# Branch b's eight output panels as seven products of halves per pair, in a one-layer streaming encoder

## The chip, the cores and the metric

The kernel runs on one core of a Trainium2 chip. The metric is the device time of one execution in microseconds (us), the median of several runs. The engines are TensorE (PE, with its weight loads PEld), VectorE (DVE), ScalarE (ACT), GpSimd (POOL), and SyncE (SP), whose queue issues most DMAs. An instruction waits in its engine's queue until what it needs is there, and all behind it wait with it.

## The reference

One layer with two branches. T = 1088 tokens (a prompt of 1024 and 64 sampled tokens), D = 1024 channels, all float32. Branch a gives `ya` (convolution, gated linear recurrence), branch b gives `yb` (forgetting attention). What the change concerns is the merge:

```python
ya = ya * jax.nn.silu(ga)
yb = yb.reshape(B, L, W_B) * jax.nn.silu(gb)
u = jnp.einsum('bsnw,nwd->bsnd', jnp.stack([ya, yb], axis=2), w_branch)
gates = jax.nn.sigmoid(jnp.stack([ma, mb], axis=2))
mix = jnp.sum(gates * u, axis=2) @ w_o
h = x + rms_norm(mix, g_post)
```

Each branch is multiplied by its own 1024 x 1024 matrix, gated per channel, the two are added, and the sum is multiplied by `w_o`.

## The kernel before

Activations lie transposed: channels on the 128 partitions in eight blocks (KT = 8), tokens along the free axis. An output panel is 128 output channels for all 1088 tokens, in three chunks of 368, 368 and 352 columns, each in one PSUM bank. Every float32 operand is split into a high and a low part (`wh`, `wl` for weights, `yah`, `yal` for inputs): ACT copies the high part, DVE subtracts it for the low part. A product is then three matmuls (`three`, L165 to L167: high by high, high by low, low by high), so a panel takes 3 chunks x 8 blocks x 3 = 72 matmuls.

Earlier in the program the q, k and gate panels are made differently. Two panels together are a product of 2 x 2 block matrices (halves of the tokens, of the input channels), made with seven products of halves instead of eight, as in Strassen's scheme in Winograd's form. One such product is 24 matmuls of 272 columns (L809, tile `quad`); POOL and DVE make the sums of the weights' halves (`split_pair`) and of the inputs' halves. Branches a and b do not use it.

The stage around the change, in the program's order:
- Branch a: panels 0 and 1 were begun earlier and are finished first (`finish_held`), then panels 2 to 7 (`panel_steps`). I call them a0 to a7. `evac_a` (L1900) multiplies each chunk by its sigmoid gate on DVE, and SP writes it to DRAM (`d_mix`).
- After each panel of a, `branch_b(of)` (L1870) makes one of the eight blocks of branch b's input: two loads, a sigmoid on ACT, a product on POOL (L1877), one on DVE (L1878), then the split into `ybh` and `ybl`.
- Branch b: eight panels of the same kind. `evac_b` gates each chunk, adds branch a's (`ma_in`, loaded from `d_mix`) and splits the sum into `mxh` and `mxl` in SBUF.
- `w_o` (`w_part`, 512 columns for each of nine blocks of tokens, the k-rows in two halves) reads `mxh` and `mxl`; then the last stage.

Weights come in pairs of panels (1 MB, four DMAs) into one raw buffer `w_raw` and are split a panel at a time into two rotating buffers (`wh`, `wl`). TensorE's order is the order of the code. In this stage a scheduler places the instructions of the other engines, from its own costs, and each engine then runs its list in order.

Of the kernel before, what the change touches and what calls it, by code (L numbers as in the profile page):

```python
# [67 lines left out]
def hybrid_step(tc, a, o):  # L68
# [31 lines left out]
    d_mix = dram.tile([KT, P, T], F32, name="d_mix")  # L100
    d_q = dram.tile([2, NP, P, T], F32, name="d_q")
# [107 lines left out]
    wpool = sb("wpool", bufs=2)  # L209

# [22 lines left out]
    for k in range(KT):  # L233
# [3 lines left out]
                  + [(w_br[i * D:(i + 1) * D, k * P:(k + 2) * P], ((t, k), (t, k + 1)))  # L237
                     for i, t in enumerate("ab") for k in range(0, KT, 2)])
# [574 lines left out]
    def keys_out(p, ss, c0, t0, blocks):  # L813
# [8 lines left out]
        for i, n in enumerate(blocks):  # L822
            n_st[0] += 1
            st = (wpool.tile([P, GC], F32, name="st") if n_st[0] % 3 else
# [1038 lines left out]
    xpool.close()  # L1863


    ybpool = sb("ybpool")
    yb = [tuple(ybpool.tile([P, T], F32R, name=f"yb{i}{k}") for i in "hl") for k in range(KT)]
    p4 = sb("p4", bufs=2)

    def branch_b(k):  # L1870
# [6 lines left out]
        pool.tensor_tensor(out=t[:, :], in0=t[:, :], in1=z[:, :], op=ALU.mult)  # L1877
        dve.tensor_tensor(out=t[:, :], in0=t[:, :], in1=s[:, :], op=ALU.mult)  # L1878
        h, l = yb[k]
        copy_act(h[:, :], t[:, :])  # L1880
        sub(dve, l[:, :], t[:, :], f(h[:, :]))

    def gate_in(pl, src):
        g = pl.tile([P, T], F32, name="gate", tag="gate", bufs=2)
        sp.dma_start(g[:, :], src)
        act.activation(out=g[:, :], in_=g[:, :], func=AF.Sigmoid)
        return g


    look_ahead()  # L1890
    split_next(dve, [t[:, :KT * P].rearrange("p (k n) -> p k n", k=KT) for t in yb[KT - 1]])
    g_next = gate_in(p4, d_ma[0])
    for of in range(KT):
        g = g_next
        if of + 1 < KT:
            g_next = gate_in(p4, d_ma[of + 1])

        def evac_a(c, t0, n, z):
            s = wpool.tile([P, GC], F32, name="st")
            dve.tensor_tensor(out=s[:, :n], in0=z, in1=g[:, t0:t0 + n], op=ALU.mult)  # L1900
# [4 lines left out]
        else:  # L1905
            tag, w = panel()
            assert tag == ("a", of)
            run(panel_steps(mm, *w, ya, evac_a))
        branch_b(of)
        if of == 2:  # L1910
            ft_p = mm.tile([P, 512], F32, name="ft_p", tag="acc")
            pe.transpose(ft_p[:64, :P], fin.rearrange("p s k -> p (s k)"), ident[:, :])
            ft = p4.tile([64, P], F32, name="ft", bufs=1)
            dve.tensor_copy(ft[:, :], ft_p[:64, :P])
# [4 lines left out]
    p4.close()  # L1919
    ypool.close()  # L1920

    NH2 = 2
    HW = D // NH2
    KH = KT // 2
    wq0 = sb("wq0", side="right")
    mxpool = sb("mxpool", side="right")
    p5 = sb("p5")
    mix = [tuple(mxpool.tile([P, T], F32R, name=f"mx{i}{of}") for i in "hl") for of in range(KT)]

    def mix_in(of):  # L1930
        g = gate_in(p5, d_mb[of])
        m = p5.tile([P, T], F32, name="ma_in", tag="ma_in", bufs=2)
        sp.dma_start(m[:, :], d_mix[of])
        return g, m

    def room_of(pl, raws, src, h, kh):

        wh = pl.tile([P, KH, HW], F32R, name="wqh", tag="wqh")
        wl = pl.tile([P, KH, HW], F32R, name="wql", tag="wql")
        for i in range(2):  # L1940
            k0 = KH * kh + 2 * i
            raw = raws[i] if raws is raw_half else raws.tile([P, KT * P], F32, name="wraw", tag="wraw", bufs=2)
            raw = raw.rearrange("p (k n) -> p k n", k=2)
            sp.dma_start(raw, src[k0 * P:(k0 + 2) * P, h * HW:(h + 1) * HW].rearrange("(k p) n -> p k n", p=P))
            ks_ = slice(2 * i, 2 * i + 2)
            copy_act(wh[:, ks_, :], raw)
            sub(dve, wl[:, ks_, :], raw, f(wh[:, ks_, :]))
        return wh, wl

    m_next = mix_in(0)  # L1950
    wo = {}
    for of in range(KT):
        g, ma_ = m_next
        if of + 1 < KT:
            m_next = mix_in(of + 1)

        def evac_b(c, t0, n, z):
            s = wpool.tile([P, GC], F32, name="st")
            c_ = slice(t0, t0 + n)
            dve.tensor_tensor(out=s[:, :n], in0=z, in1=g[:, c_], op=ALU.mult)  # L1960
            dve.tensor_tensor(out=s[:, :n], in0=s[:, :n], in1=ma_[:, c_], op=ALU.add)
            copy_act(mix[of][0][:, c_], s[:, :n])
            sub(dve, mix[of][1][:, c_], s[:, :n], f(mix[of][0][:, c_]))

        tag, w = panel()
        assert tag == ("b", of)
        if of == KT - 1:
            wo[0, 0] = room_of(wq0, raw_half, a["w_o"], 0, 0)
            wq0.tile([P, 56], F32, name="lead")
        run(panel_steps(mm, *w, yb, evac_b))  # L1970
    p5.close()
    ybpool.close()
    wpool.close()

# [3 lines left out]
    hpool = sb("hpool")  # L1978
    wq = sb("wq", bufs=3)
    tpool = sb("tpool")  # L1980
# [6 lines left out]
    wo[0, 1] = room_of(wq, tpool, a["w_o"], 0, 1)  # L1987
# [52 lines left out]
    wg = {}  # L2040
# [5 lines left out]
    def w_part(b, h, kh):  # L2046
# [4 lines left out]
        wh, wl = wo[h, kh]  # L2051
        for k in range(KH):
# [202 lines left out]
```

## Time and profile before

| | |
|---|---|
| median of 3 runs | 1424.47 us (1424.3 to 1426.01) |
| profiled execution, its span | 1425.84 us, 1424.0 us |
| TensorE clock granted | 0.998 |
| branch a's first panels finished | 1026.4 us into the span |
| branch b's first matmul | 1097.94 us |
| w_o's first matmul | 1192.66 us |

A line of a group has: source line, engine, operation, output <- inputs by name, shapes, number of instructions; then busy us and mean ns of one; then the engine's idle time before them and what ended it. A line of a timeline has: start, duration, engine, line, operation, and in brackets the idle time before it and its releaser. `SPq` is SP's queue issuing a DMA. A matmul's duration overlaps the next one's, so that rates are read from start to start.

### The profile page before, as it was taken

What the parts mean: (1) busy time and instruction counts of PE and PEld (TensorE: products, weight loads), DVE (VectorE), ACT (ScalarE), POOL (GpSimd) and SP (SyncE); (2) the same over time, 40 slices, a digit from 0 to 9 for tenths busy, and PEclk for the clock granted to TensorE, in tenths of its full rate; (3) what the DMA queues carried; (4) which work ended last, traced back from release to release, by engine and by line L of the source; (5) the groups of instructions that cost most, each with busy time, mean ns of one, the idle gap of its engine ahead of it and who ended that gap; (6) DMA issues with size and microseconds to landing.
All of it is one profiled execution on the core that took longest, in us unless ns stands there. A gap on an engine that the chain in (4) does not pass through costs nothing.

```text
span 1424.0 us, 23913 instructions
## 1 busy us (share of the span) xinstructions
PE 1407.3 (99%) x8967; PEld 1339.5 (94%) x8967; DVE 863.2 (61%) x1528; ACT 711.9 (50%) x1300; POOL 280.1 (20%) x370
## 2 busy tenths in 40 slices
PE   9999999999999999999999999999999999999997
PEld 8999999999999999999999989999999999888886
DVE  6546665665532467676676667799745544348644
ACT  5414444344321566666666657879533323324543
POOL 0001333413311333243432410010122000000001
PEclk9999999999999999999999999999999999999999
DMA  5376555656346857647465533331486534124111
GB/s 206 122 130 111 105 172 180 191 157 176 93 78 187 215 138 138 157 111 173 118 146 139 66 88 48 56 53 36 157 292 204 186 127 146 66 73 151 49 49 45
DMA packets 133552, 182.70 MB, mean 128 GB/s; under 512 B 22212, under 2 KB 97004, under 8 KB 133436
## 3 DMA queue, kind: packets, MB, share of 16 engines
q1 hardware_dynamic: 116892, 156.57, 44.0%
q10 hardware_dynamic: 16240, 23.97, 4.7%
q8 instruction: 71, 1.16, 0.3%
q0 software_dynamic: 304, 0.62, 0.1%
q14 instruction: 45, 0.37, 0.1%
HBM read 122.65 MB, written 58.46 MB: 127 GB/s over the span
## 4 chain that ended last, share of the span: by engine, by line
PE 90%; DMA 4%; DVE 3%; ACT 1%; issue 1%; SPq 0%; ACTq 0%; DVEq 0%
PE quad L809 19%; PE acc L165 15%; PE acc L166 15%; PE acc L167 15%; PE tp L1192 4%; PE s L1167 3%; PE s L1166 2%; PE pv L1221 2%; PE pv L1219 2%; DMA w_raw<-in_w_in 2%; PE vacc L165 1%; PE vacc L167 1%; PE vacc L166 1%; PE tp L2012 1%; DMA wv_raw<-in_w_in 1%
## 5 line engine op out<-in xcount | busy, mean ns | idle before, releaser
L165 PE MATMUL acc<-xh,wh 128*128 128x368 f32 (+1 forms) x672 | 227.6, 339 | 0.4
L166 PE MATMUL acc<-xl,wh 128*128 128x368 f32 (+1 forms) x672 | 219.9, 327 | 0.0
L167 PE MATMUL acc<-xh,wl 128*128 128x368 f32 (+1 forms) x672 | 219.6, 327 | 0.0
L165 PEld LDWEIGHTS acc<-xh,wh 128*128 128x128 f32 x672 | 126.4, 188 | 1.9 <-DVE nm L1146 1.3
L166 PEld LDWEIGHTS acc<-xl,wh 128*128 128x128 f32 x672 | 126.7, 189 | 0.6
L167 PEld LDWEIGHTS acc<-xh,wl 128*128 128x128 f32 x672 | 126.4, 188 | 0.0
L84 ACT ACTIVATE th<-tp 128x512 fp32r<-128x512 f32 (+1 forms) x160 | 86.7, 549 | 63.9 <-PE tp L1192 53.6
L87 DVE TENSOR_TENSOR tl<-tp,th 128x512 fp32r<-128x512 f32 (+1 forms) x160 | 99.2, 634 | 28.5 <-ACT th L84 27.4
L87 DVE TENSOR_TENSOR wl<-w_raw,wh 128x1024 fp32r<-128x1024 f32 (+1 forms) x64 | 73.0, 1140 | 60.6 <-ACT wh L84 51.2
L84 ACT ACTIVATE wh<-w_raw 128x1024 fp32r<-128x1024 f32 (+1 forms) x64 | 61.3, 959 | 94.9 <-PE quad L809 38.3
L1152 POOL TENSOR_SCALAR pb<-pb,sm 128x640 f32<-128x640 f32 (+1 forms) x64 | 61.6, 962 | 168.5 <-DVE sm L1151 153.4
L809 PE MATMUL quad<-xh,wh 128*128 128x272 f32 x448 | 94.0, 291 | 0.0
L809 PE MATMUL quad<-xl,wh 128*128 128x272 f32 x448 | 92.6, 288 | 0.0
L809 PE MATMUL quad<-xh,wl 128*128 128x272 f32 x448 | 92.5, 288 | 0.0
L1149 ACT ACTIVATE pb<-pb,nm 128x640 f32<-128x640 f32 (+1 forms) x64 | 63.3, 989 | 25.7 <-DVE nm L1146 17.7
L1219 PE MATMUL pv<-tl,vv 128*128 128x512 f32 x192 | 70.0, 365 | 2.1 <-DVE y L1231 1.3
L809 PEld LDWEIGHTS quad<-xl,wh 128*128 128x128 f32 x448 | 70.6, 188 | 0.0
L809 PEld LDWEIGHTS quad<-xh,wh 128*128 128x128 f32 x448 | 70.3, 188 | 0.2
L809 PEld LDWEIGHTS quad<-xh,wl 128*128 128x128 f32 x448 | 70.4, 188 | 0.0
L1166 PE MATMUL s<-k,q 128*128 128x128 f32 (+2 forms) x192 | 67.3, 358 | 0.0
L1146 DVE CUSTOM_DVE_ANT_0 pb<-s,mask 128x640 f32<-128x640 f32 (+1 forms) x64 | 64.8, 1013 | 3.8 <-PE s L1167 3.4
L1167 PE MATMUL s<-k,q 68*128 68x128 f32 (+2 forms) x192 | 64.5, 348 | 0.0
(560 smaller groups left out, 3829.5 us busy)
## 6 DMA issues: line engine op xcount, KB each, us to landing
w_raw<-in_w_in SPq DMA_DIRECT2D x56, 256.0 KB
q<-d_q SPq DMA_DIRECT2D x48, 256.0 KB
k<-d_k SPq DMA_DIRECT2D x48, 256.0 KB
w_raw<-in_w_branch SPq DMA_DIRECT2D x32, 256.0 KB
w_raw<-in_w_in SPq DMA_DIRECT2D x56, 128.0 KB
wraw<-in_w_in SPq DMA_DIRECT2D x24, 256.0 KB
d_k<-oh ACTq DMA_DIRECT2D x16, 272.0 KB
d_k<-kl SPq DMA_DIRECT2D x16, 272.0 KB
```

The source lines that it names most:

```text
L84: return act.activation(out=out, in_=in_, func=AF.Copy, scale=scale)
L87: return eng.tensor_tensor(out=out, in0=in0, in1=in1, op=ALU.subtract)
L165: pe.matmul(out, ah, bh, start=start, stop=False)
L166: pe.matmul(out, ah, bl, start=False, stop=False)
L167: pe.matmul(out, al, bh, start=False, stop=stop)
L809: pe.matmul(acc[:, c, :CW], l[:, k, :], r[:, k, c * CW:(c + 1) * CW], start=(first and k == 0 and p == 0), stop=(k == 3 and p == 2), skip_ ...
L1146: at = book("D", now[0] + HOP_PE, per(D_MAX, n), lambda: dve.tensor_tensor_reduce(out=pr[:, :n], in0=s[:, :n], in1=m, scale=-1.0, scalar=- ...
L1149: at = book("A", at, per(A_EXP, n), lambda: act.activation(out=pr[:, :n], in_=pr[:, :n], func=AF.Exp, scale=-1.0, bias=nm, accum_out=sm))
L1152: return free, book("G", at, per(G_NORM, n), lambda: pool.tensor_scalar(out=pr[:, :n], in0=pr[:, :n], scalar1=sm, scalar2=1.0, op0=ALU.mul ...
L1166: pe.matmul(s[:, c0:c0 + w], t["q1"][:, q], t["k1"][:, c0:c0 + w], start=True, stop=False)
L1167: pe.matmul(s[:, c0:c0 + w], t["q2"][:HD + 4, q], t["k2"][:HD + 4, c0:c0 + w], start=False, stop=True)
L1219: pe.matmul(pv[:, 512 - n:], v, tl[:, c:c + n], start=(j == 0), stop=False)
```

## The change

Branch b's eight panels become four pairs of seven products of halves.
- `branch_b(k)` now makes blocks k and k + 4 together, and out of them the inputs of the products: the plain quarters B11 and B21 with their splits, and the sums T1 to T4 and B22 unsplit, in ten tiles t0 to t9. It runs after panels a2 (twice), a3 and a4. One of the sums (`t3` in the code) is POOL's.
- Panel a7 is written with its k-steps outermost, in the order 3, 4, 0, 7, 6, 5, 1, 2, and its three accumulators open together. From there on ACT's and DVE's order is the code's (`manual_schedule`).
- After a7's matmuls t0 to t7 are split (`split_t`, 1088 columns each, ACT and DVE), a part of the first pair's weights (`next(splits)`), and then a7's three chunks are evacuated.
- The seven products (`product_b`) go to four PSUM tiles of two banks. `put_b` adds, gates (DVE), adds branch a's part (POOL) and writes the mixed half panel to DRAM (`d_mx`). `mix_room` loads it again, `split_mix` splits it for w_o.
- Gates are loaded and opened by halves of the tokens. w_o's and the last stage's weight buffers move between pools.

The diff, cut to the lines that the prediction speaks of:

```diff
@@ branch_b
+        t, s = gated(k)
         dve.tensor_tensor(out=t[:, :], in0=t[:, :], in1=s[:, :], op=ALU.mult)
-        h, l = yb[k]
-        copy_act(h[:, :], t[:, :])
-        sub(dve, l[:, :], t[:, :], f(h[:, :]))
+        u, s = gated(k + 4)
+        t2, t1, t3, t4, b22 = (raw_t[2 * i + k // 2][:, k % 2, :] for i in range(5))
+        dve.tensor_tensor(out=b22, in0=u[:, H[1]], in1=s[:, H[1]], op=ALU.mult)
+        dve.tensor_tensor(out=u[:, H[0]], in0=u[:, H[0]], in1=s[:, H[0]], op=ALU.mult)
+        b11, b12, b21 = t[:, H[0]], t[:, H[1]], u[:, H[0]]
+        for x, h, l in ((b11, b11h, b11l), (b21, b21h, b21l)):
+            h, l = (y[k // 2][:, k % 2, :] for y in (h, l))
+            copy_act(h, x)
+            sub(dve, l, x, f(h))
+        sub(dve, t1, b12, b11)
+        sub(pool, t3, b22, b12)
+        sub(dve, t2, b22, t1)
+        sub(dve, t4, b21, t2)
@@ the loop over branch a's panels
+            s = p5.tile([P, HT], F32, name="s", tag="s", bufs=2)
...
-            run(panel_steps(mm, *w, ya, evac_a))
-        branch_b(of)
+            if of == KT - 2:
+                load_b(0)
+                splits = split_pair(0, panels(b_raw[0]), w_b[0])
+            if of < KT - 1:
+                run(panel_steps(mm, *w, ya, evac_a))
+            else:
+                seq = tc.manual_schedule(engines={act.engine, dve.engine})
+                seq.__enter__()
...
+                next(splits)
+                next(splits)
+                next(splits)
+                wh, wl = w
+                accs_ = [mm.tile([P, 512], F32, name="acc", tag="acc") for _ in CH]
+                ks = (3, 4, 0, 7, 6, 5, 1, 2)
+                for k in ks:
+                    for c, (t0, n) in enumerate(CH):
+                        three(accs_[c][:, :n], wh[:, k, :], wl[:, k, :], ya[k][0][:, t0:t0 + n], ya[k][1][:, t0:t0 + n],
+                              k == ks[0], k == ks[-1])
+        for k in {2: (0, 1), 3: (2,), 4: (3,)}.get(of, ()):
+            branch_b(k)
...
+    mm.close()
+    psq = ps("psq_b", bufs=4)
...
+    load_b(1)
+    for _ in range(3):
+        next_m()
+    for i in range(8):
+        split_t(i)
+    next(splits)
+    for c, (t0, n) in enumerate(CH):
+        evac_a(c, t0, n, accs_[c][:, :n])
...
+    def put_b(of, h, z, in1):
...
+        dve.tensor_tensor(out=s3, in0=z, in1=in1, op=ALU.add)
+        dve.tensor_tensor(out=s[:, :], in0=s[:, :], in1=g[:, :], op=ALU.mult)
+        pool.tensor_tensor(out=s[:, :], in0=s[:, :], in1=m[:, :], op=ALU.add)
+        sp.dma_start(d_mx[of][:, H[h]], s[:, :])
...
+    for i in range(4):
+        w, first, last = w_b[i], i == 0, i == 3
...
+        ta, za = bank()
+        product_b(ta, w["a11"], B11, True)
+        p1_ = part("p1_")
+        copy_act(p1_, za)
```

How this moves instructions, by the lists of the engines. In these rows `acc` are accumulators of ordinary panels, `quad_b` those of the new products, `gate` branch a's gates, `wh`/`wl` split weights, and what stands in brackets is what the instruction waits for: the names of semaphores, one for each engine and DMA queue.

TensorE where branch b begins, before: the last matmuls of a7 and the first of panel b0, which waits for ACT's copy of weights.

```order
L165 MATMUL acc_12947<-yah7_12248,wh_12785 128x352
L166 MATMUL acc_12947<-yal7_12249,wh_12785 128x352
L167 MATMUL acc_12947<-yah7_12248,wl_12786 128x352
L165 MATMUL acc_13030<-ybh0_12276,wh_12887 128x368 [waits Activation_49]
L166 MATMUL acc_13030<-ybl0_12277,wh_12887 128x368
L167 MATMUL acc_13030<-ybh0_12276,wl_12888 128x368 [waits DVE_49]
```

The same place after: the last matmuls of a7 (its k-step 2) and the first product.

```order
L166 MATMUL acc_12994<-yah2_10462,wh_12874 128x352
L167 MATMUL acc_12994<-yal2_10463,wh_12874 128x352
L168 MATMUL acc_12994<-yah2_10462,wl_12875 128x352
L2079 MATMUL quad_b_13146<-b0_12284,wh_12982 128x272 [waits DVE_49,Activation_49]
L2079 MATMUL quad_b_13146<-b0_12284,wh_12982 128x272
L2079 MATMUL quad_b_13146<-b2_12286,wh_12982 128x272 x2
```

The panel's first matmul waited for ACT alone; the first product's first matmul waits for DVE too, up to the evacuation of a7's third chunk, `s_13138` in the rows below, on whose bank its tile lies.

DVE around the end of branch a, before: the last three evacuations of branch a stand among splits of weights and of branch b's inputs.

```order
L1878 TENSOR_TENSOR yb_in_12975<-yb_in_12975,gb_s_12977 128x1088 [waits Activation_49,Pool_49]
L1900 TENSOR_TENSOR st_12846<-acc_12821,gate_12681 128x368 [waits DMAHW3_49,PE_49]
L87 TENSOR_TENSOR ybl7_12291<-yb_in_12975,ybh7_12290 128x1088 [waits Activation_49]
L1900 TENSOR_TENSOR st_12874<-acc_12849,gate_12681 128x352 [waits DMAHW1_49,PE_49]
L87 TENSOR_TENSOR wl_12888<-w_raw_102,wh_12887 128x1024 [waits DMAHW6_49,DMAHW5_49,DMAHW7_49,DMAHW0_49,Activation_49]
L1900 TENSOR_TENSOR st_12916<-acc_12891,gate_12782 128x368 [waits DMAHW2_49,DVE_49,PE_49]
L1900 TENSOR_TENSOR st_12944<-acc_12919,gate_12782 128x368 [waits DMAHW3_49,DVE_49,PE_49]
L1900 TENSOR_TENSOR st_12972<-acc_12947,gate_12782 128x352 [waits DMAHW4_49,DVE_49,PE_49]
L87 TENSOR_TENSOR wl_13023<-w_raw_102,wh_13022 128x1024 [waits Activation_49]
L1960 TENSOR_TENSOR st_13055<-acc_13030,gate_13012 128x368 [waits DVE_49,DMAHW5_49,PE_49,Activation_49]
```

DVE there after, from the fourth of eight splits on (t0l, t1l and t2l stand directly ahead, and before them the first pair's weights, `wl_12983` and `wl8_12987`):

```order
L87 TENSOR_TENSOR t3l_13085<-t3_12460,t3h_13084 128x1088 [waits DVE_49,Activation_49]
L87 TENSOR_TENSOR t4l_13087<-t4_12461,t4h_13086 128x1088 [waits DVE_49,Activation_49]
L87 TENSOR_TENSOR t5l_13089<-t5_12462,t5h_13088 128x1088 [waits DVE_49,Activation_49]
L87 TENSOR_TENSOR t6l_13091<-t6_12463,t6h_13090 128x1088 [waits DVE_49,Activation_49]
L87 TENSOR_TENSOR t7l_13093<-t7_12464,t7h_13092 128x1088 [waits DVE_49,Activation_49]
L87 TENSOR_TENSOR wl_13126<-s1_12975,wh_13125 128x512 [waits PE_49,Activation_49]
L87 TENSOR_TENSOR wl_13126<-w_raw_106,wh_13125 128x512 [waits Activation_49]
L1960 TENSOR_TENSOR s_13131<-acc_12992,gate_12868 128x368 [waits DMAHW3_49]
L1960 TENSOR_TENSOR s_13134<-acc_12993,gate_12868 128x176 [waits DMAHW5_49]
L1960 TENSOR_TENSOR s_13134<-acc_12993,gate_12871 128x192
L1960 TENSOR_TENSOR s_13138<-acc_12994,gate_12871 128x352 [waits DMAHW1_49,DVE_49]
L2091 TENSOR_TENSOR s_13205<-quad_b_13180,p1__13171 128x544 [waits DVE_49,DMAHW2_49,PE_49,Activation_49]
```

Between the first pair's weights and a7's evacuation (`s_13131` to `s_13138`) now stand eight splits of 1088 columns and two of 512; the first output's add (L2091) follows.

DVE where a6's weights are split (`wl_12685`), before:

```order
L87 TENSOR_TENSOR wl_12580<-w_raw_102,wh_12579 128x1024 [waits Activation_49]
L1900 TENSOR_TENSOR st_12612<-acc_12587,gate_12475 128x368 [waits DMAHW5_49,DVE_49,PE_49]
L1878 TENSOR_TENSOR yb_in_12566<-yb_in_12566,gb_s_12568 128x1088 [waits Activation_49,Pool_49]
L1900 TENSOR_TENSOR st_12640<-acc_12615,gate_12475 128x368 [waits DMAHW7_49,DVE_49,PE_49]
L87 TENSOR_TENSOR ybl3_12283<-yb_in_12566,ybh3_12282 128x1088 [waits Activation_49]
L1900 TENSOR_TENSOR st_12668<-acc_12643,gate_12475 128x352 [waits DMAHW5_49,PE_49]
L87 TENSOR_TENSOR wl_12685<-w_raw_102,wh_12684 128x1024 [waits DMAHW3_49,DMAHW2_49,DMAHW4_49,DMAHW1_49,Activation_49]
```

The same place after (a6's weights are `wl_12780`):

```order
L87 TENSOR_TENSOR t3_12460<-yb_in_12620 128x544 [waits DVE_49]
L1960 TENSOR_TENSOR s_12712<-acc_12687,gate_12525 128x176 [waits DMAHW0_49,PE_49]
L1895 TENSOR_TENSOR t9_12466<-yb_in_12628,gb_s_12630 128x544 [waits Activation_49,Pool_49]
L1896 TENSOR_TENSOR yb_in_12628<-yb_in_12628,gb_s_12630 128x544
L87 TENSOR_TENSOR b3_12287<-yb_in_12620,b1_12285 128x544 [waits Activation_49]
L87 TENSOR_TENSOR t1_12458<-t9_12466,t3_12460 128x544 [waits DVE_49]
L87 TENSOR_TENSOR b7_12291<-yb_in_12628,b5_12289 128x544 [waits Activation_49]
L87 TENSOR_TENSOR t7_12464<-yb_in_12628,t1_12458 128x544 [waits DVE_49]
L1960 TENSOR_TENSOR s_12712<-acc_12687,gate_12528 128x192
L1960 TENSOR_TENSOR s_12741<-acc_12716,gate_12528 128x352 [waits DMAHW7_49,PE_49]
L87 TENSOR_TENSOR wl_12780<-w_raw_106,wh_12779 128x1024 [waits DMAHW5_49,DMAHW4_49,DMAHW6_49,DMAHW3_49,Activation_49]
L1960 TENSOR_TENSOR s_12808<-acc_12783,gate_12645 128x368 [waits DMAHW1_49,DVE_49,PE_49]
```

Before, one block's product (`yb_in`) and split (`ybl3`) stood between the evacuations ahead of the split; now it is all of a double block.

More of the change, by code (lines that the diff above doesn't have):

```diff
@@ L1924, in hybrid_step @@
     KH = KT // 2
[L1925 to L1939, printed above, removed]
-        for i in range(2):
[L1941 to L1970, printed above, removed]
+    wo, wg = {}, {}
@@ L2050, in w_part @@
         acc = w_accs[b]
[L2051 to L2052 removed]
+        for k, (wh, wl) in enumerate(wo[h, kh]):
             k_ = KH * kh + k
```

244 lines of the change are left out of this document (206 added, 38 removed).

## The prediction

> **What bounds the kernel now.** I read the page's head and its chain first, then the rows of TensorE at both ends of branch b, then the windows around branch a's end, and last the prices.
>
> ```profile
> span 1424.0 us, 23913 instructions
> PE 1407.3 (99%) x8967; PEld 1339.5 (94%) x8967; DVE 863.2 (61%) x1528; ACT 711.9 (50%) x1300; POOL 280.1 (20%) x370
> PE 90%; DMA 4%; DVE 3%; ACT 1%; issue 1%; SPq 0%; ACTq 0%; DVEq 0%
> ```
>
> PE (TensorE) is the bound: busy 99% of the span and 90% of the chain. Less arithmetic there shortens the kernel one for one, and every microsecond in which PE newly waits lengthens it. So the question is which waits the change makes. The profiled run is 1425.84 us, 1.84 outside the span; the median, 1424.47, is 1.37 lower. I work out a difference against the trace and add it to the median. A difference under 0.2% (2.8 us) can't be told from none.
>
> ```profile
> 1097.94 0.33 PE L165 MATMUL acc<-ybh,wh 128*128 128x368 f32 x1
> 1098.11 0.33 PE L166 MATMUL acc<-ybl,wh 128*128 128x368 f32 x1
> ...
> 1192.50 0.32 PE L167 MATMUL acc<-ybh,wl 128*128 128x352 f32 x1
> 1192.66 0.40 PE L165 MATMUL acc<-wqh,mxh 128*128 128x512 f32 x1
> 1192.89 0.39 PE L166 MATMUL acc<-wql,mxh 128*128 128x512 f32 x1
> ```
>
> Branch b starts at 1097.94 and w_o at 1192.66: 94.72 us, 11.84 for each of eight panels. A new 368-column matmul starts every 0.17, a 352-column one every 0.16 (1192.50 to 1192.66), a 512-column one every 0.23. The chain has what a product of halves costs:
>
> ```profile
> 295.62 27.06 PE quad L809 x216
> ...
> 339.92 111.27 PE quad L809 x888
> ```
>
> 216 matmuls are nine products, 888 are 37: 3.007 us each, 37 of them without a break.
>
> ```profile
> 1022.00:1046.00 24.00, 24.00 (x147) 23.95 (x146) 14.03 (x18) 11.38 (x11) 7.71 (x3) 1.00 0.75 247
> 1046.00:1070.00 24.00, 24.00 (x148) 24.00 (x147) 10.47 (x13) 9.56 (x9) 5.14 (x2) 1.00 0.90 310
> 1070.00:1094.00 24.00, 24.00 (x147) 24.00 (x147) 16.12 (x15) 9.62 (x10) 9.53 (x3) 1.00 0.68 213
> 1094.00:1118.00 24.00, 24.00 (x148) 24.00 (x147) 9.84 (x17) 7.22 (x9) 0.00 (x0) 1.00 0.56 199
> ```
>
> The columns are the window, then PE, PEld, DVE, ACT and POOL, the granted clock, the DMA share and GB/s. While branch a's panels run, PE never stops, DVE is 10 to 16 of 24 us busy, and the DMA engines reach 0.90.
>
> **The prices of the added work**, all from one profile:
>
> ```profile
> L87 DVE TENSOR_TENSOR wl<-w_raw,wh 128x1024 fp32r<-128x1024 f32 x14 | 17.1, 1222 | 3.6 <-ACT wh L84 3.6
> L1878 DVE TENSOR_TENSOR yb_in<-yb_in,gb_s 128x1088 f32<-128x1088 f32 x8 | 10.3, 1289 | 10.9 <-POOL yb_in L1877 10.9
> L1900 DVE TENSOR_TENSOR st<-acc,gate 128x368 f32<-128x368 f32 x12 | 6.4, 535 | 4.1 <-PE acc L167 3.8 <-DMA d_mix<-st 0.3
> L87 DVE TENSOR_TENSOR wl<-wraw,wh 128x512 fp32r<-128x512 f32 x10 | 7.0, 696 | 0.0
> L913 DVE TENSOR_TENSOR u__2291<-quad,p__2158 128x544 f32<-128x544 f32 x1 | 0.7, 726 | 0.1
> L1877 POOL TENSOR_TENSOR yb_in<-yb_in,gb_in 128x1088 f32<-128x1088 f32 x8 | 22.4, 2798 | 89.6 <-ACT gate L1886 49.7 <-DMA gb_in<-d_gb 35.2 <-DMA yb_in<-d_y 4.6
> L669 POOL TENSOR_TENSOR s<-w_raw 128x512 f32<-128x512 f32 x4 | 6.3, 1572 | 34.8 <-DVE wl L87 34.8
> L84 ACT ACTIVATE ybh<-yb_in 128x1088 fp32r<-128x1088 f32 x8 | 8.9, 1109 | 13.0 <-DVE yb_in L1878 13.0
> ```
>
> **Fewer matmuls: a gain.** Four pairs of seven products are 28 × 3.007 = 84.2 us in place of 94.7: −10.5 us, if PE waits no more than now.
>
> **The first product of branch b.** This is the step that I think decides. Branch b's first PSUM tile lies on the banks of two of panel a7's accumulators, the third chunk's among them. So the first matmul waits for DVE to evacuate that chunk. In DVE's order this evacuation now stands behind the eight splits t0l to t7l, behind two halves of a weight split, and behind the other two chunks; before, nothing but ordinary panel work stood there. With S the start of t0l, the third chunk is out after 8 × 1.29 = 10.3, 2 × 0.70 = 1.4, the first chunk 0.54, and then the release of its staging buffer, which the third chunk reuses (two buffers):
>
> ```profile
> 1045.30 0.35 SPq L1901 DMA_DIRECT2D d_mix<-st  x1
> ...
> 1047.29 0.54 DVE L1900 TENSOR_TENSOR st<-acc,gate 128x368 f32<-128x368 f32 x1 [0.28 <-DMA d_mix<-st]
> ```
>
> That took 1.99 from issue to release, in which the middle chunk fits; the last chunk adds 0.53. Altogether PE restarts at S + 14.8. ACT's copies (1.11 each) run ahead of DVE's 1.29 and cost nothing more. Everything queued behind on DVE, first the first output's add, waits too.
>
> S has two bounds. It can't come before the place of t0l is free, which branch a's third k-step frees: five of eight k-steps before the panel's end E, each 6 × 0.167 + 3 × 0.160 = 1.48, so E − 7.4. And DVE's order puts pair 0's weight splits ahead of t0l. Their raw weights go into the buffer of a7's weights:
>
> ```profile
> 1101.11 2.34 SPq L247 DMA_DIRECT2D w_raw<-in_w_branch  x4
> ...
> 1111.16 1.06 ACT L84 ACTIVATE wh<-w_raw 128x1024 fp32r<-128x1024 f32 x1 [3.15 <-DMA w_raw<-in_w_branch]
> ```
>
> Such a load took 10.05 us to use. If a7's weights are split just in time (E − 11.85), the load ends at E − 1.8, POOL's three sums (3 × 1.57) at E + 2.9, ACT's copy (half of 1.06) and DVE's two halves (1.4) at E + 4.8. So the wait is 7.4 to 19.6 us. I take S = E + 1.5, a wait of 16.3, nearer the late end, because DVE has to share:
>
> ```profile
> 1081.75 3.19 POOL L1877 TENSOR_TENSOR yb_in<-yb_in,gb_in 128x1088 f32<-128x1088 f32 x1 [1.68 <-DMA yb_in<-d_y]
> ...
> 1082.57 3.52 DVE L87 TENSOR_TENSOR ybl<-yb_in,ybh 128x1088 fp32r<-128x1088 f32 x1
> ```
>
> A DVE subtraction that takes 1.29 alone took 3.52, ending 1.1 us after the POOL product beside it.
>
> **Branch b's inputs, moved and swollen.** Eight calls spread over eight panels become four double ones, issued after a2, a2, a3 and a4. Each asks POOL for 2 × 2.80 and a sum of half the size (1.40), 7.0 together, and DVE for 1.29 and seven halves of 0.70, 6.2. Three stand ahead of a6's weight split in DVE's order. In the 47.4 us of a2 to a5: POOL 21.0, DVE 18.6, four weights 4.9, fifteen evacuations 8.0; 52.5 if the two engines exclude each other throughout, 5.1 too many, and no wait if they don't. The loads of the same calls (eight of 1088 KB), crowded into four panels beside weights and gates, pull the same way in a stretch that is at 0.90. I take 4.0 of the 0 to 5.1 for PE's wait at a6.
>
> [...]
>
> **Inside branch b.** For each pair (21.0 us) DVE has six PSUM reads of 0.73, four gates of 0.70 and 4.7 of weight splits, 11.9; POOL four weight sums of 1.57 and four adds of 1.40, 11.9. One after the other that is 2.8 too much a pair (upper bound 8 over three pairs), side by side nothing. The nearest row is the 37 products without a break, with the same weight sums: 0. Evacuations' ACT copies and second halves of splits go away; ACT isn't near its limit.
>
> **To DRAM and back.** The last output's add (0.73), gate (0.70), POOL (1.40), write (1.99) and reload come before its split (1.11 + 1.29).
>
> ```profile
> 1110.57 0.34 SPq L1885 DMA_DIRECT2D gate<-d_mb  x1
> ...
> 1114.31 1.11 ACT L1886 ACTIVATE gate<-gate 128x1088 f32<-128x1088 f32 x1 [1.70 <-DMA gate<-d_mb]
> ```
>
> With 3.74 for the reload (a gate of the same size) the split ends 11 us after the last product, 15 with another split and two weights ahead of it. Six blocks of w_o's first half, 72 × 0.23 = 16.6 us, hide it; their k-rows 0 to 3 came back earlier. I take 0, and some 3 if SP's queue delays it. w_o's first accumulator, though, waits for that add to leave the bank:
>
> ```profile
> PE wake L440 <- POOL ident L113: 1.6, 1, 1.6
> ...
> PE quad L809 <- DVE u__1656 L896: 0.9, 1, 0.9
> ```
>
> 0.9, as a product waited for such an add; the first row is PE's longest wait of all now, so no long stop is on show.
>
> **Restarting TensorE.** At the kernel's start PE comes out of rest:
>
> ```profile
> 1.60 5.08 PE L440 MATMUL wake<-ident 128*128 128x128 f32 x28 [1.60 <-POOL ident L113]
> 6.61 0.23 PE L439 MATMUL g_p<-ident,g 8*128 8x8 f32 x1
> ...
> 7.31 2.05 PE L413 MATMUL tp<-dg,x_in 128*128 128x128 f32 x16
> ```
>
> 28 transposes took 5.01, where 16 later took 2.05 (0.128 each): 1.4 us lost. A 16-us stop may cost 0 to 1.4; I take 1.4. [...] No run here shows a stop in mid-kernel.
>
> **Sum.** −10.5 + 16.3 + 4.0 + 0 + 0 + 0.9 + 1.4 = +12.1 us: 1437.9 against the profiled run, **1436.6** against the median.
>
> **Rivals.**
> 1. *The splits are early (not slower).* DVE and POOL don't collide, the weights are ahead, and S = E − 7.4: the wait is 7.4, a6 waits 0. −10.5 + 7.4 + 0.9, and 0 to 1.4: 1422.3 to 1423.7. It decides as soon as S comes before E − 6.6, where the wait and the last two terms equal 10.5. For it: DVE is only 10 to 16 of 24 us busy. Against it: the 3.52 row, and that load and three sums have to be done 13 us sooner than just in time.
> 2. *No wait at all at branch b's start (the gain is kept).* 1414 to 1415. It needs the first product to find its banks free; against it is DVE's order.
> 3. *Everything late.* 19.6 and 5.1, and 3 for the reload or branch b's POOL: −10.5 + 19.6 + 5.1 + 3 + 0.9 + 1.4 = +19.5: 1444. The loads at 0.90 speak for it, PE's unbroken rows now against it.
> 4. *DVE and POOL take turns inside branch b*: up to 8 more than the sum, of which I count 4: 1440.6.
>
> **Chances.** The sum's case 0.55 (its own range 1430 to 1443); rival 1 0.15 (faster by over 0.2% in a third of it, none in the rest); rival 2 0.05; rival 3 0.15; rival 4 0.10. Faster 0.10, same 0.10, slower 0.80. The range 1421 to 1445 leaves out rival 2 and the far sides of 3 and 4.
>
> **What would show it.** Right: one PE wait of 10 to 20 us before the first product, released by DVE, with t0l to t7l and the evacuations of a7 inside it; a smaller one before a6's first or second matmul, released by ACT or DVE; seven products in 21.0 us; w_o's first matmul 0.9 late. Wrong: a first product that follows a7 within 7 us (S was early), waits between products (rival 4), or a wait at w_o's k-row 6 (the reload).

## The result and the profile after

The changed kernel takes 1448.21 us (median of 4 runs, 1446.49 to 1451.01), the kernel before, run beside it, 1424.72 (4 runs, 1424.3 to 1426.01). The ratio is 1.0165 [1.0146, 1.0184]: 23.5 us slower. The direction was forecast, the size was not: 1436.6 was the forecast and 1445 the end of its range.

The head of the page, the slices of TensorE with its granted clock, and the chain's shares, of the kernel after:

```profile
span 1444.8 us, 24360 instructions
...
PE 1406.2 (97%) x9063; PEld 1334.1 (92%) x9063; DVE 910.0 (63%) x1554; ACT 726.2 (50%) x1330; POOL 347.3 (24%) x406
...
PE   9999999999999999999999999999986999999997
...
PEclk9999999999999999999999999999988999999999
...
PE 91%; DVE 4%; DMA 3%; issue 1%; POOL 1%; ACT 1%; SPq 0%; DVEq 0%; POOLq 0%; ACTq 0%
```

PE was busy for 1407.3 us before and for 1406.2 now: the saved arithmetic (10.5 by the forecast) is not there as busy time. One part of the reason stands in the slices: in the two of 36 us each (1444.8 / 40) from about 1047 to 1120 us, where a6, a7 and the seam of the branches lie, PE is less busy, and in the same two its clock is down, to 0.88 and 0.83. A matmul at the lower clock counts as busy for longer (0.51 us for 0.33 in a6's rows below). The other part, slower matmuls in the last stages, doesn't show in the slices; it comes further down. PE's waits, with their total, number and longest:

```profile
PE quad_b L2079 <- DVE s L1960: 16.6, 1, 16.6
PE acc L166 <- ACT wh L84: 3.2, 1, 3.2
PE acc L168 <- DVE wl L87: 2.8, 1, 2.8
...
PE acc L166 <- DVE s__14100 L2091: 0.7, 1, 0.7
```

These are the forecast waits, at the forecast places: before branch b's first product, at a6 (two), and before w_o's first matmul. PE around the middle of them, from a7's last matmul to the first product, and at branch b's end:

```profile
1105.48 0.32 PE L168 MATMUL acc<-yah,wl 128*128 128x352 f32 x1
...
1122.44 1.24 PE L2079 MATMUL quad_b<-b,wh 128*128 128x272 f32 x4 [16.64 <-DVE s L1960]
...
1208.18 0.41 PE L2079 MATMUL quad_b<-t9h,wl 128*128 128x272 f32 x2
1209.29 0.47 PE L166 MATMUL acc<-wh,mxh 128*128 128x512 f32 x1 [0.69 <-DVE s__14100 L2091]
```

With these starts the two traces divide into stages, in us:

| stage | before | after | difference |
|---|---|---|---|
| up to a2's first matmul | 1026.54 | 1024.55 | -1.99 |
| a2's first matmul to branch b's first | 71.40 | 97.89 | +26.49 |
| branch b's first matmul to w_o's first | 94.72 | 86.85 | -7.87 |
| w_o's first matmul to the end | 231.34 | 235.51 | +4.17 |
| span | 1424.0 | 1444.8 | +20.8 |

The first row varies between 1023.7 and 1026.5 in all the kernels below, whose work is the same up to there; I don't count it as the change's. In the second, 16.64 + 3.22 + 2.84 are the waits, and 3.8 are left. In the third, 10.5 were saved by forecast, 0.69 is the wait at w_o, and some 2 are missing. The fourth was not forecast at all. So three things had to be explained besides the waits: the 3.8, the 2 and the 4.17.

*The 3.8 and the 2: TensorE after a stop.* a6's first matmuls:

```profile
1075.56 0.68 PE L166 MATMUL acc<-yah,wh 128*128 128x368 f32 x1 [3.22 <-ACT wh L84]
1076.04 0.51 PE L167 MATMUL acc<-yal,wh 128*128 128x368 f32 x1
1079.39 0.68 PE L168 MATMUL acc<-yah,wl 128*128 128x368 f32 x1 [2.84 <-DVE wl L87]
1079.86 0.51 PE L166 MATMUL acc<-yah,wh 128*128 128x368 f32 x1
1080.17 0.51 PE L167 MATMUL acc<-yal,wh 128*128 128x368 f32 x1
...
1085.07 0.39 PE L168 MATMUL acc<-yah,wl 128*128 128x368 f32 x1
1085.30 0.33 PE L166 MATMUL acc<-yah,wh 128*128 128x368 f32 x1
1085.47 0.33 PE L167 MATMUL acc<-yal,wh 128*128 128x368 f32 x1
```

From start to start they take 0.31 (1079.86 to 1080.17) where 0.17 is normal (1085.30 to 1085.47). From 1075.56 to 1085.30 stand 21 matmuls: 9.74, less the wait of 2.84, is 6.90, against 21 x 0.167 = 3.51. That is 3.4 of the 3.8. The granted clock says the same; windows of 2 us (start:end, length, then busy time of PE, PEld, DVE, ACT and POOL, the clock, DMA share, GB/s):

```profile
1080.00:1082.00 2.00, 2.00 (x8) 2.00 (x7) 0.54 (x1) 0.00 (x0) 0.00 (x0) 0.50 0.85 311
...
1086.00:1088.00 2.00, 2.00 (x14) 2.00 (x13) 1.97 (x2) 1.70 (x3) 1.75 (x1) 1.00 1.04 395
...
1124.00:1126.00 2.00, 2.00 (x11) 2.00 (x11) 0.00 (x0) 0.00 (x0) 0.00 (x0) 0.50 0.65 194
1126.00:1128.00 2.00, 2.00 (x17) 2.00 (x17) 0.00 (x0) 0.60 (x2) 0.00 (x0) 0.96 0.00 0
```

PE is busy for all of each window, but at 0.50 it starts 8 matmuls of a6 where it starts 14 at 1.00, and 11 of branch b where it starts 17 at 0.96.

*The 4.17: slower matmuls in the last stages.* The same group of 512-column matmuls, first before, then after:

```profile
L165 PE MATMUL acc<-wqh,mxh 128*128 128x512 f32 x128 | 49.9, 390 | 0.0
```
```profile
L166 PE MATMUL acc<-wqh,mxh 128*128 128x512 f32 x96 | 38.0, 396 | 0.0
...
L167 PE MATMUL acc<-wql,mxh 128*128 128x512 f32 x96 | 38.0, 395 | 0.0
```

Each takes 5 to 6 ns longer. There are no waits in this group and the clock is 1.00. The w_o and last-stage weights, which here are the moving operand, now begin at another place in SBUF: `wqh` at byte 138976 of each partition, 32 past a multiple of 64, where it was at 60672, a multiple of 256 (the places, here and below, are from the builds' memory maps; the traces don't hold them).

### The profile page after: what moved, and what is told of

The parts are those of the page before. It is cut to its first block, busy times and chain, and to the rows that moved or that the text cites. A ratio compares the mean times of both kernels' runs of the same rounds, so it can differ in the third digit from the quotient of the medians.

```text
span 1444.8 us, 24360 instructions
## 1 busy us (share of the span) xinstructions
PE 1406.2 (97%) x9063; PEld 1334.1 (92%) x9063; DVE 910.0 (63%) x1554; ACT 726.2 (50%) x1330; POOL 347.3 (24%) x406
## 4 chain that ended last, share of the span: by engine, by line
PE 91%; DVE 4%; DMA 3%; issue 1%; POOL 1%; ACT 1%; SPq 0%; DVEq 0%; POOLq 0%; ACTq 0%
PE quad L810 19%; PE acc L166 13%; PE acc L167 13%; PE acc L168 13%; PE quad_b L2079 5%; PE tp L1193 4%; PE s L1168 2%; PE s L1167 2%; PE pv L1222 2%; PE pv L1220 2%; PE vacc L457 1%; PE vacc L166 1%; DMA w_raw<-in_w_in 1%; PE vacc L167 1%; PE vacc L168 1%
## 5 line engine op out<-in xcount | busy, mean ns | idle before, releaser
L87 DVE TENSOR_TENSOR wl<-w_raw,wh 128x1024 fp32r<-128x1024 f32 (+1 forms) x67 | 78.9, 1179 | 59.4 <-ACT wh L84 52.9
L84 ACT ACTIVATE wh<-s 128x512 fp32r<-128x512 f32 x54 | 34.1, 631 | 93.9 <-PE quad L810 61.5
```

What stands on the lines that cost most here:

```text
L84: return act.activation(out=out, in_=in_, func=AF.Copy, scale=scale)
L87: return eng.tensor_tensor(out=out, in0=in0, in1=in1, op=ALU.subtract)
```

## Experiments

Four theories came out of this. *Arrears* (work that an engine is behind with): the 16.6 us are DVE's list between branch a's end and a7's third evacuation. *Clock*: behind a stop PE runs for a while at the clock of 0.50 (0.31 us from start to start for 0.17), and that is the 3.8 and the 2. *Address*: the 4.17 are the place of the weights. *a6*: its two waits come from branch b's doubled input work. The rivals: TensorE's new products are slower in themselves; the stages behind branch b suffer from the DRAM round trip; a6 starves by total DVE and POOL time.

| kernel | a2 to branch b | branch b | w_o to the end | median, us |
|---|---|---|---|---|
| before | 71.40 | 94.72 | 231.34 | 1424.0 to 1424.7 |
| after | 97.89 | 86.85 | 235.51 | 1448.21 |
| e1_pad224 | 97.97 | 87.57 | 231.68 | 1444.49 |
| e3_evac_first | 86.31 | 94.01 | 235.77 | 1443.15 |
| e5_warm | 98.46 | 85.15 | 235.58 | 1445.49 |
| e6_late | 95.39 | 87.18 | 235.58 | 1444.91 |
| e11_dve | 91.28 | 87.95 | 235.48 | 1443.14 |
| e8_all | 78.15 | 91.19 | 232.25 | 1430.49 |
| e12_best | 72.39 | 89.02 | 231.80 | 1420.46 |

**The address, moved back (e1) and moved away in the kernel before (e2).** A tile that nothing uses, ahead of the weights' pool: 224 bytes in the kernel after (`wqh` to 138752, a multiple of 256), 32 bytes in the kernel before (`wqh` to 60704).

```diff
# e1_pad224, against after
+    hpool.tile([P, 56], F32, name="lead6")
# e2_before_off32, against before
+    hpool.tile([P, 8], F32, name="lead6")
```

> The changed kernel with one unused tile of 224 bytes, so that the weight tiles wqh and wql of w_o and of the last stage start at a multiple of 256 bytes (138752) as before the change, and not at 138976, 32 past a multiple of 64. From w_o's first matmul to the end of the span the changed kernel took 235.5 us, before 231.3, with no wait in either. Address theory: the moving operand's start address slows each 512-column matmul from 0.229 to 0.234 us; this stage falls back to 231.3 to 231.8, and the run is 4 us shorter than the changed kernel, about 1444 (median). Rival (the part of the memory, or the neighbours' work, slows the matmuls): the stage stays at 235 to 236 and the time at 1447 to 1449. Both: the waits ahead of w_o stay at 16 to 17, 3 and 3 us.

> The kernel before the change with one unused tile of 32 bytes ahead of wq, so that most of its wqh and wql tiles start 32 bytes past a multiple of 64. Address theory: the stage from w_o's first matmul to the end takes 234 to 235.5 us in place of 231.3, and the run is 3 to 4 us longer than before, 1427.5 to 1429. Rival: no change, 1424 to 1425.5.

e1: 1444.49, ratio to before 1.0137 [1.0122, 1.0152]; w_o to the end 231.68, where the kernel before has 231.34. The waits stayed. e2: 1427.63, ratio 1.0023 [1.0014, 1.0033]; w_o to the end 234.14, 2.8 longer than before. Its pad moved most of the weight tiles, not all. The group's row, in e1 and then in e2:

```profile
L166 PE MATMUL acc<-wqh,mxh 128*128 128x512 f32 x96 | 37.4, 390 | 0.0
```
```profile
L165 PE MATMUL acc<-wqh,mxh 128*128 128x512 f32 x128 | 50.6, 395 | 0.0
```

390 ns where the weights lie at a multiple of 256, 395 where they don't, in either kernel. In e1 `mxh`, the other operand of these matmuls, is allocated from another pool, which the pad doesn't move. So the loss hangs on the weights' place, and the DRAM round trip has no part in these 3.8 of the 4.17 us; the other 0.3 are not located.

**How coarse the rule is (e7, e9).** The same tile with 8 and 24 floats: `wqh` at 138944, a multiple of 64 but not of 128, and at 138880, a multiple of 128 but not of 256.

```diff
# e7_pad32 / e9_pad96, against after
+    hpool.tile([P, 8], F32, name="lead6")
# or
+    hpool.tile([P, 24], F32, name="lead6")
```

> The changed kernel with an unused tile of 32 bytes in place of 224, so that wqh and wql start at a multiple of 64 that is none of 256 (138944). If 64 is what counts: w_o's first matmul to the end takes 231.5 to 232 us and the run about 1444.5, as with 224 bytes. If 256 is: 235 to 236, and about 1448.

> The changed kernel with an unused tile of 96 bytes, so that wqh and wql start at 138880, a multiple of 128 and not of 256. 32 bytes (a multiple of 64) left w_o's first matmul to the end at 235.6 us, 224 bytes (a multiple of 256) gave 231.7. If 128 is enough: 231.5 to 232; if 256 is needed: 235.5.

Neither helped: 1447.5 (ratio 1.0163) and 1447.68 (one run), w_o to the end 235.59 and 235.13, the group at 395 and 396 ns. Of the places tried, only the multiples of 256 (60672 and 138752) gave 390 ns. It is no general rule for moving operands: the sums t0 to t9, 272 columns each, begin at 224 past a multiple of 256 by the same maps, and branch b's 28 products run at the rate of the earlier ones all the same (3.016 us each for 3.007, e5 below). Why, is open.

**DVE's arrears (e3).** a7's three evacuations go ahead of the eight splits.

```diff
+    for c, (t0, n) in enumerate(CH):
+        evac_a(c, t0, n, accs_[c][:, :n])
     for i in range(8):
         split_t(i)
     next(splits)
-    for c, (t0, n) in enumerate(CH):
-        evac_a(c, t0, n, accs_[c][:, :n])
```

> The changed kernel with a7's three evacuations ahead of the eight splits in ACT's and DVE's order, nothing else. Order theory (the first product waits for its bank alone): the wait of 16.6 us before the first product falls to 4 to 8 (the third chunk still waits some 3 us for a staging buffer's write), nothing new of size appears, and the run is 9 to 12 us shorter than the changed kernel, 1436 to 1439. Arrears theory (DVE has to do the splits in any case): the first wait falls to 4 to 8 as well, but the products that read t4 to t7 or the tile that the third product shares wait 5 to 9 us in its place; the run is 2 to 6 us shorter, 1442 to 1446.

1443.15, ratio 1.0131 [1.0115, 1.0146]. PE's waits:

```profile
PE quad_b L2079 <- DVE s L1960: 5.0, 1, 5.0
PE quad_b L2079 <- DVE u__13248 L2142: 4.4, 1, 4.4
```

The wait fell by 11.6, from 16.6 to 5.0: so much of it was the order of the list. But the splits now stand ahead of the first outputs' adds, a wait of 4.4 appears inside branch b, and PE restarts slowly a second time there (two matmuls of 272 columns in 0.45 us at 1129.65, for 0.25 from 1132.63 on): branch b takes 94.01. Of 11.6 us gained at the seam, 7.2 are given back.

**Keeping PE busy through the stop (e5).** 90 matmuls of 368 columns into a bank that is free, between a7 and the first product. They compute nothing that is used.

```diff
+        if of == KT - 1:
+            warm = mm.tile([P, 512], F32, name="acc", tag="acc")
+            bh = b11h[0][:, 0, :]
+            for j in range(90):
+                pe.matmul(warm[:, :368], bh[:, :P], bh[:, :368], start=True, stop=True)
```

> The changed kernel with 90 matmuls of 368 columns between a7's panel and the first product, into an unused PSUM bank that nobody reads: they fill about 15 of the 16.6 us in which TensorE waits. Clock theory (TensorE runs at half rate after a long rest): the first products run at 0.125 us a matmul from the start, the granted clock stays at 1.00 there, and the time from the first product to w_o's first matmul falls from 86.9 to 84.9 us; the run is about 2 us shorter than the changed kernel, about 1446. Rival (the slow first matmuls come from something else that the wait leaves behind, such as cold operands): 86.9 stays and so does the time. The wait at a6 and its slow matmuls stay in both.

1445.49, ratio 1.0148 [1.0133, 1.0163]. The first product, and the window behind it:

```profile
1123.77 0.73 PE L2084 MATMUL quad_b<-b,wh 128*128 128x272 f32 x4 [1.95 <-DVE s L1960]
```
```profile
1124.00:1126.00 2.00, 2.00 (x18) 2.00 (x18) 0.00 (x0) 0.00 (x0) 0.00 (x0) 1.00 0.96 321
```

The first product starts 1.33 us later in the span than in the kernel after (1123.77 for 1122.44), and yet branch b is 1.70 shorter: four matmuls take 0.73 instead of 1.24, at clock 1.00. So the loss in branch b was the clock after the stop. Less w_o's 0.69, the 28 products take 84.46, 3.016 each, for the 3.007 of the products earlier in the program: they are not slower in themselves.

**Branch b's input work later (e6), or off POOL (e11).** e6 moves the last two double blocks to behind a4 and a5. e11 leaves the code's order and moves one instruction of each block from POOL to DVE.

```diff
# e6_late
-        for k in {2: (0, 1), 3: (2,), 4: (3,)}.get(of, ()):
+        for k in {2: (0, 1), 4: (2,), 5: (3,)}.get(of, ()):
...
-        if of == 4:
+        if of == 5:
# e11_dve
-        pool.tensor_tensor(out=t[:, :], in0=t[:, :], in1=z[:, :], op=ALU.mult)
+        dve.tensor_tensor(out=t[:, :], in0=t[:, :], in1=z[:, :], op=ALU.mult)
```

> The changed kernel with the third and fourth call of branch_b issued one panel of branch a later (after a4 and a5). Theory: a6's weights are late because the third call's rows stand ahead of them on ACT and DVE; so the two waits at a6 (3.2 and 2.8 us) shrink to under 1 in all and its slow matmuls (3.8 us) go, but the fourth call runs into the splits, so that the wait before the first product grows from 16.6 by 2 to 4. Net 5 to 8 us shorter than the changed kernel, about 1441 to 1443. Rival (a6's weights are late because their load or the weight buffer is late): the waits at a6 stay, and the time stays or grows.

> The changed kernel with the product of branch_b (yb_in by gb_in, 1088 columns, 2.54 us on POOL) on DVE (1.29 us), nothing else. Exclusion theory: a POOL instruction holds DVE up for its whole length, so that DVE loses more to POOL's product than the product costs DVE itself; branch_b's chain gets shorter, a6's weights come in time, and the two waits at a6 (6.0 us) with its slow matmuls (3.8) go; the wait before the first product stays at 15 to 19, since the splits still stand ahead of the evacuation. About 10 us shorter than the changed kernel, 1437 to 1440. Rival (DVE's own sum of work is what is too much): eight more products of 1.29 make a6 later still, by up to 8 us in all, 1448 to 1456.

e6: 1444.91, ratio 1.0143 [1.0129, 1.0157]. e11: 1443.14, ratio 1.013 [1.0116, 1.0144]. Both gained less than was expected of them, 3.3 and 5.1 us. The rival of total time would have made e11 worse, since DVE gets more work; that of a late load or weight buffer would have left a6's waits in e6. a6's waits went in both, but for 0.7 and 0.5. In the kernel after, the rows that lead to them are these, of POOL, DVE and ACT (ACT's and DVE's instructions that a6's waits name are at the end of the last two groups):

```profile
1065.43 2.54 POOL L1885 TENSOR_TENSOR yb_in<-yb_in,gb_in 128x1088 f32<-128x1088 f32 x1 [5.15 <-DMA yb_in<-d_y]
1068.86 2.86 POOL L1885 TENSOR_TENSOR yb_in<-yb_in,gb_in 128x1088 f32<-128x1088 f32 x1 [0.88 <-DMA yb_in<-d_y]
```
```profile
1068.01 1.29 DVE L1892 TENSOR_TENSOR yb_in<-yb_in,gb_s 128x1088 f32<-128x1088 f32 x1 [4.30 <-POOL yb_in L1885]
...
1069.84 2.46 DVE L87 TENSOR_TENSOR t<-yb_in 128x544 f32<-128x544 f32 x1
...
1078.13 1.21 DVE L87 TENSOR_TENSOR wl<-w_raw,wh 128x1024 fp32r<-128x1024 f32 x1
```
```profile
1073.91 0.66 ACT L84 ACTIVATE b<-yb_in 128x544 fp32r<-128x544 f32 x1 [1.81 <-DVE yb_in L1896]
1074.47 1.04 ACT L84 ACTIVATE wh<-w_raw 128x1024 fp32r<-128x1024 f32 x1
```

It is a chain in order of time, not a sum of busy times: a load arrives late, POOL multiplies, DVE stands idle 4.30 us for POOL, then ACT stands idle 1.81 for DVE, and behind ACT's copy of `yb_in` stands the copy of a6's weights. In the pair 1068.86 (POOL, 2.86) and 1069.84 (DVE, 0.7 alone, 2.46 here) the two also get in each other's way: DVE ends 0.6 after POOL and has lost 1.7. How the 6.06 divide into idle time handed on and such losses isn't separated; e11 takes both away. With POOL out of it, DVE of e11 does the same product in 1.29 us, for POOL's 2.54:

```profile
1063.64 1.29 DVE L1885 TENSOR_TENSOR yb_in<-yb_in,gb_in 128x1088 f32<-128x1088 f32 x1 [1.19 <-DMA yb_in<-d_y]
1064.85 0.72 DVE L87 TENSOR_TENSOR t<-yb_in 128x544 f32<-128x544 f32 x1
```

Both gained less than the waits that they took away, since the next wait grew. In e6:

```profile
PE quad_b L2079 <- DVE s L1960: 22.6, 1, 22.6
...
PE acc L168 <- DVE wl L87: 0.7, 1, 0.7
```

Of 6.06 of waits and 3.4 of slow clock at a6, 0.7 was left, and 5.9 came back at the bank. In e11 that wait is 18.7, 2.1 more, and branch b took 1.1 longer (6.18 us of its work fell into the low clock behind the stop, where the kernel after has 3.72). DVE had arrears at branch a's end anyway; part of what a6 no longer waits for is waited for there.

**All of it together (e8, e12).** e8: the pad of e1; a7's evacuations first, the third chunk with a buffer of its own; the splits spread over the first pair's products; the double blocks behind a0, a2, a4 and a5. For the blocks to come so early, the first weights are split into other tiles (t1 and t3), and the tiles of the sums are made as they are needed. Weight splits of branch a were given priority in the scheduler.

```diff
...
-        for k in {2: (0, 1), 3: (2,), 4: (3,)}.get(of, ()):
+        for k in {0: (0,), 2: (1,), 4: (2,), 5: (3,)}.get(of, ()):
...
-    for i in range(8):
-        split_t(i)
-    next(splits)
     for c, (t0, n) in enumerate(CH):
         evac_a(c, t0, n, accs_[c][:, :n])
+    split_t(0)
+    split_t(1)
+    next(splits)
+    split_t(2)
+    split_t(3)
...
-            split_t(8)
-            split_t(9)
+            split_t(4)
+            split_t(5)
...
+            split_t(6)
+            split_t(7)
...
+            split_t(8)
+            split_t(9)
...
+    hpool.tile([P, 56], F32, name="lead6")
```

> The changed kernel with all of it mended that the runs so far name: the 224 bytes; the calls of branch_b spread over panels a0, a2, a4 and a5, with high priority for the panels' weights; a7's evacuations ahead of the splits, the third through a staging buffer of its own; the splits of the sums between the first products, each shortly ahead of the product that reads it. If DVE's place in the order and the address are all that was lost: no wait at a6, 4 to 7 us before the first product, 4 to 6 us in smaller waits among the first seven products, slow matmuls for 2 to 4 us, and -10.5 from the products: 1424 to 1430, as long as before the change or a little longer. If DVE's and POOL's sum of work bounds the stretch in any order, the waits only move: 1434 or more.

1430.49, ratio 1.0046 [1.0032, 1.006], half a microsecond above what was expected: a6 doesn't wait, but the first product still does, 6.5. e12 is e8 with e11's product on DVE, the blocks behind a0, a2, a3 and a4, no priority, and t5's split one place later:

```diff
# against e8
-        for k in {0: (0,), 2: (1,), 4: (2,), 5: (3,)}.get(of, ()):
+        for k in {0: (0,), 2: (1,), 3: (2,), 4: (3,)}.get(of, ()):
...
-        pool.tensor_tensor(out=t[:, :], in0=t[:, :], in1=z[:, :], op=ALU.mult)
+        dve.tensor_tensor(out=t[:, :], in0=t[:, :], in1=z[:, :], op=ALU.mult)
...
```

> The run with all mended, and the product of branch_b on DVE as well; the calls stand after a0, a2, a3 and a4, without the high priority, and the split of t5 comes after the second sum. Exclusion theory: the wait of 6.5 before the first product falls under 3, too short for a slow restart; 3 to 5 us of small waits stay among the first two pairs' products; -10.5 from the products: 1419 to 1423, shorter than before the change. If DVE's own work bounds: no better than the run with all mended, 1430.

1420.46 (10 runs, 1418.9 to 1421.92), ratio 0.9972 [0.9963, 0.9982]: 3.9 us faster than the kernel before. Which of its four differences from e8 brought the last 10 us isn't separated. Its waits around branch b:

```profile
PE quad_b L2084 <- DVE t8l L87: 1.4, 1, 1.4
...
PE quad_b L2084 <- DVE s__13116 L1963: 0.7, 1, 0.7
PE quad_b L2084 <- DVE s L2096: 0.3, 1, 0.3
```

Its first product starts at 1097.98, where the kernel before had its first matmul at 1097.94. It has not all of the 10 us: branch b takes 89.02, not 85.15. 1.7 of the 3.9 are waits (1.4 and 0.3; the 0.7 stands ahead of the first product). Behind the stop of 1.4, which began at 1117.02, the clock was at 0.50 for 3.41 us, and half of that, an estimate from the clock, is another 1.7:

```profile
1119.08:1122.49 3.41, 3.41 (x16) 3.29 (x15) 3.39 (x3) 0.00 (x0) 0.47 (x1) 0.50 0.58 183
1123.00:1126.00 3.00, 3.00 (x26) 3.00 (x25) 3.00 (x4) 0.52 (x1) 1.69 (x1) 1.00 0.41 111
```

16 matmuls run in the 3.41 us at 0.50, 26 in the 3.00 us at 1.00. So the expectation that a wait under 3 is too short for a slow restart did not hold.

## Why the prediction was wrong in size

Three steps failed: the price of restarting TensorE, +1.4, measured 5.1; the weights' new place, which got no term, cost 4.17; and a6's wait, +4.0 with a bound of 5.1, was 6.06. The terms of the sum, against the trace (us):

| term | predicted | measured | from |
|---|---|---|---|
| 28 products for 94.7 | -10.5 | -10.3 | 84.46 in e5 |
| wait before the first product | +16.3 | +16.64 | PE's waits |
| a6's wait | +4.0 | +6.06 | 3.22 + 2.84 |
| inside branch b | 0 | 0 | no wait in it |
| DRAM and back | 0 | 0 | e1, and no wait at w_o's k-rows |
| w_o's bank | +0.9 | +0.69 | PE's waits |
| restarting TensorE | +1.4 | +5.1 | 3.4 at a6, 1.7 in branch b |
| weights moved between pools | not priced | +4.17 | 3.8 of it undone by e1 |
| not located, a2 to branch b | | +0.4 | 3.8 - 3.4 |
| ahead of a2 | | -2.0 | stage table |

The right column sums to the 20.8 between the spans. Between the medians there are 2.7 more. The profiled run of the kernel after is the shortest of its four, the others are 0.7 to 4.5 longer; why they spread so much more than those of the kernel before stays open, but for some 1.4 us at most that the clock can account for (below).

**The change's gain and its main wait: right.** The working of the 16.3 was right only in its sum. DVE's rows around branch a's end E (1105.64):

```profile
1104.49 1.55 DVE L87 TENSOR_TENSOR wl<-w_raw,wh 128x512 fp32r<-128x512 f32 x1
1105.97 1.28 DVE L87 TENSOR_TENSOR t0l<-t,t0h 128x1088 fp32r<-128x1088 f32 x1
...
1115.72 1.29 DVE L87 TENSOR_TENSOR t7l<-t,t7h 128x1088 fp32r<-128x1088 f32 x1
...
1118.13 1.04 DVE L1960 TENSOR_TENSOR s<-acc,gate 128x368 f32<-128x368 f32 x3
1121.77 0.52 DVE L1960 TENSOR_TENSOR s<-acc,gate 128x352 f32<-128x352 f32 x1 [2.59 <-DMA d_mix<-s]
```

S, the start of t0l, came directly behind the pair's weight split, as in the prediction's late bound, but at E + 0.3 and not E + 1.5; and from S to the restart passed 16.5, not 14.8: the splits follow each other by 1.39 (seven steps from 1105.97 to 1115.72), not by 1.29, and the staging buffer's release (SP issued the write at 1118.76, the third chunk starts at 1121.77) took 3.0, not 1.99. The two errors cancel: that 16.3 is so close to 16.64 is luck.

**a6's wait: mechanism half right, size over its bound.** The step bounded it by busy times, 52.5 in 47.4, at most 5.1. The 6.06 came down a chain, from a load to POOL to DVE to ACT, with idle time at each link, and a sum of busy times can't bound that. The lower bound, no wait at all if POOL and DVE don't exclude each other, did not hold either: the rows at 1068.86 and 1069.84 show DVE held up beside POOL (2.46 us for 0.71).

**Restarting TensorE: the size was wrong, over its bound.** The step took the kernel's start as its row, 1.4 for one stop, and gave a6 nothing. In mid-kernel the stop ahead of branch b cost 1.7 and a6's stops 3.4. The clock's own stretches at 0.50 say the same. In the kernel after:

```profile
1074.96:1085.20 10.24, 6.79 (x21) 6.32 (x22) 5.75 (x11) 2.61 (x3) 2.58 (x2) 0.50 0.78 257
1109.09:1126.16 17.07, 3.72 (x16) 3.75 (x17) 10.09 (x12) 4.95 (x7) 4.13 (x3) 0.50 0.63 204
```

PE ran for 6.79 us of the first and 3.72 of the second, and half of each, 3.4 and 1.9, is lost, an estimate from the clock. In e1, whose program is the same up to w_o, it is 1.8 and 2.6:

```profile
1077.57:1084.39 6.82, 3.68 (x12) 3.68 (x13) 3.79 (x7) 0.70 (x1) 0.63 (x1) 0.50 0.86 282
1108.29:1128.77 20.48, 5.12 (x22) 5.15 (x23) 12.06 (x14) 7.13 (x9) 4.13 (x3) 0.50 0.60 198
```

In mid-kernel these stretches lasted 3.41 us or a multiple of it (10.24 and 17.07 in the kernel after, 6.82 and 20.48 in e1, 3.41 in e12), and how much of the work falls into them changes from trace to trace. So the price of a stop has a spread: by this reckoning the two places together cost 4.4 us in e1, 4.6 in e9, 5.3 in the kernel after and 5.8 in e7, all with the same code there. That the stop at branch b cost 1.7 is one case of it: 2.6 in e1. The length of a stop did not sort those of these runs: 1.4 us in e12 brought the clock down, 1.95 in e5 did not.

**The weights' place: the step that is missing.** The edit stood in the change's description and got no price. It made w_o and the last stage 4.17 longer, as much as a6's wait was forecast to be.

Of the rivals, none came: S was not early, branch b's engines did not collide, the reload was hidden. The upper one had 1444 for 19.6, 5.1 and 3 us of waits; the time lies above it with smaller waits, for the two reasons just given.

## What to carry to other kernels

When a change makes the bounding engine stop, read the clock and the start-to-start times behind the stop too: here stops of 16.6 us and of 3.2 and 2.8 us cost 5.1 more in matmuls at the clock of 0.50. A wait that was removed while the engine behind it had arrears came back in part at that engine's next deadline: 7.2 of 11.6 us in e3, 5.9 at the bank in e6, 2.1 in e11. The change paid only in e12, where the splits were spread and POOL's product had moved; e8, with the splits spread and the product still on POOL, was 0.5% slower than the kernel before. And an edit that only moves buffers belongs in the sum: compare where the matmuls' operands begin before and after.

## What the runs showed of the hardware

- A 512-column matmul whose moving weights begin at a multiple of 256 bytes in the partition took 390 ns in the rows (before, e1); at the places tried between it took 395 to 396 (remainders of 32 in e2, 128 in e9, 192 in e7 and 224 in the kernel after, modulo 256 by `wqh`), about 4 us for this kernel (places from the memory maps). Matmuls of 272 columns on sums at a remainder of 224 lost nothing that shows: 3.016 us a product for 3.007 (e5). The exact rule is open.
- TensorE's granted clock was 1.00 or 0.50, and in mid-kernel it stayed at 0.50 for 3.41 us or a multiple of it: 3.41 (e12), 6.82 and 20.48 (e1), 10.24 and 17.07 (after). It came down with stops of 16.6 us and of 3.2 (after) and with one of 1.4 (e12); it stayed up through stops of 1.95 (e5), 1.80 (e8) and 1.35 us (at 828 us of the kernel after). So the length of a stop alone doesn't decide; what does is open.
- POOL took 2.53 to 2.86 us (after) for a 128x1088 product that DVE did in 1.29 (e11); with it on DVE, PE's waits of 6.06 at a6 fell to 0.5 although DVE had more to do (busy for 38.94 us of the 46 from 1030 on, for 29.89).
- Of the DVE instructions that started while such a POOL product ran, in the kernel after, those with both inputs in SBUF were stretched (a 1088-column one from 1.29 to 3.62 us at 1052.40, 544-column ones from 0.71 to 2.46 at 1069.84 and to 3.09 at 1086.30); the evacuations, which read one input from PSUM, were not (0.54 at 1069.38).
